# First mixer, latents: sums of squares on VectorE, heads' norms written later, conditioning pieces at program order

## Chip, cores and metric

The kernel runs on one core of a Trainium2 chip. The metric is the device time of one execution, in microseconds (us). The kernel before was timed three times; its median is 1766.79 us. The engines are called by the names that the profile uses: PE (TensorE), DVE (VectorE), ACT (ScalarE), POOL (GpSimd) and SP (SyncE, which here only issues DMAs).

## What is computed

The reference is a diffusion backbone of two layers over 512 latent and 256 context tokens (768 together), with a model width of 1024. The first layer mixes tokens with two kinds of attention side by side: multi-head latent attention and grouped-query attention. Cut to what matters here:

```python
def rmsnorm(x, g):
    return x * lax.rsqrt(jnp.mean(x * x, axis=-1, keepdims=True) + EPS) * g

# conditioning: 6 x 1024 values per layer, each a dot product of length 1024
mod = jnp.dot(jax.nn.silu(c), ada_w[layer]) + ada_b[layer]
# one input projection, cut into: latent q (384), latent kv (256), k_rope (32),
# grouped-query q (512), k (128), v (128)
cq, ckv, kr, gq, gk, gv = split_cols(jnp.dot(h, w_in), EVEN_SPLITS)
q = apply_rope(rmsnorm(gq per head of 64, g_gq))       # 8 heads
k = apply_rope(rmsnorm(gk per head of 64, g_gk))       # 2 heads
# the latents cq and ckv are normalised over their whole width, then projected up
```

After the mixer comes a gated feed-forward block, then the second layer; the output is the latent stream.

## The kernel before, in words

Matrices are multiplied in three passes: each operand is split into a rounded high part and a remainder (`split`, L39: ACT copies the high part at L42, DVE subtracts at L43), and high x high, low x high and high x low are summed in PSUM. Weights come in pieces of at most 1024 columns (`weights`, L59): a DMA from SP's queue into a raw tile `wr` (two buffers), then `wh` on ACT and `wl` on DVE (three buffers each). A raw buffer is free again when its `wl` is made.

The tile framework puts the instructions of each engine (and the DMAs of SP's queue) into a fixed order before the run: among those whose inputs are ready in its plan it takes the one with the best priority, and the priority is the place in the program text unless a block changes it. `ada_piece` (L128) wraps its work in `high_priority(offset=-100000)`; `_ada_piece` (L132) is the same work without the wrapper. One conditioning piece loads 512 KB into a tile `ar` (three buffers, L135), makes two products with row sums on DVE (tiles `junk`, L138, 128x1024 each, one for the latent and one for the context condition) and one small add (L139).

The stretch of the change lies in the first 160 us. `first_norm` (L152, its loop over slices at L241) normalises the input, walks over eight slices k of the width (L221 to L223 make `u`, `hh` and `hl`), runs pieces 12 to 15 for k = 0 to 3 by `_ada_piece`, and accumulates the six 128-token tiles of the grouped-query q in PSUM. Then `even` (L550) goes through these steps in the program text:

1. For six tiles t: `fill()` (L584), which takes one of the pieces 16 to 31; the square on ACT (L586); the rotary products on DVE (L573, L577, from PSUM) with an add on POOL (L581); a sum per head on DVE (L588). The result is `QR`.
2. The weights for k and v, `in_w_gkv`, 288 columns, in three pieces of 3, 3 and 2 slices (L589).
3. For six tiles t: the matmuls into a bank of T, U, R (L592, `tm`, L95), `fill()` (L593), then the same treatment for `KR`, and the split of v (L594 to L601).
4. The inverse root of 60 means per token on DVE (L603, L604): `rg`.
5. Six times: scale `QR[t]` (L607) and `KR[t]` (L609) by `rg` on POOL.
6. For the five column groups c of the latents: weights (`in_w_lat`, L623), 48 matmuls into one of two PSUM buffers `lat` (L626, L85), two `fill()` (L629, L630), the square on ACT into `sa` or `sq` (L632, L635), the add of `sq` to `sa` for c = 1, 2 and 4 (L636, on POOL but for c = 4, one `sq` buffer), and the split into `CQ` or `CK` (L637). The sums over the width are matmuls (L620), at c = 4 and after the loop.
7. Attention: `kprep` transposes `KR` (L680), the q preparation transposes `QR` (L703).

The sixteen pieces are used up by the first twelve `fill()` of steps 1 and 3 and the four of c = 0 and 1.

Of the kernel before, what the change touches and what calls it, by code (L numbers as in the profile page):

```python
# [9 lines left out]
F32 = mybir.dt.float32  # L10
# [7 lines left out]
SUB, ADD, MUL, MAX, MIN = ALU.subtract, ALU.add, ALU.mult, ALU.max, ALU.min  # L18

D = 1024  # L20
NL, NX, T = 512, 256, 768
# [11 lines left out]
class Kernel:  # L33
# [516 lines left out]
    def even(self, hh, hl, acc):  # L550
        nc, i, tc = self.nc, self.i, self.tc
# [4 lines left out]
        TP = tc.alloc_tile_pool(name="inp", bufs=1, reuse_waits="tile", side="right")  # L556
        rest = list(range(16, 32))

        def fill():
            if rest:  # L560
                self.ada_piece(0, rest.pop(0))


        QR = P1.tile([128, 6, 512], F32, tag="QR", name="QR")
        KR = P1.tile([128, 6, 128], F32, tag="KR", name="KR")
# [17 lines left out]
        for t in range(6):  # L583
            fill()  # L584
            sq = TP.tile([128, 512], F32, tag="gsq", name="gsq", bufs=2)
            nc.scalar.square(sq, acc[t])  # L586
            ropemul(QR[:, t], acc[t], Cq, Sq, 8, t)
            nc.vector.tensor_reduce(ssg[:, t, 0:8], sq.rearrange("p (h d) -> p h d", h=8), axis=AX.X, op=ADD)  # L588
        wkv = self.weights(i["w_gkv"], KD, 288)  # L589
        for t in range(6):  # L590
            ps = self.B("TUR")
            self.tm(ps[:, 0:288], wkv, H, KD, t)  # L592
            fill()  # L593
            sq = TP.tile([128, 512], F32, tag="gsq", name="gsq", bufs=2)  # L594
            nc.scalar.square(sq[:, 0:128], ps[:, 0:128])
            ropemul(KR[:, t], ps[:, 0:128], Ck, Sk, 2, t)
            nc.vector.tensor_reduce(ssg[:, t, 8:10], sq[:, 0:128].rearrange("p (h d) -> p h d", h=2), axis=AX.X, op=ADD)
            vs = ps[:, 128:256].rearrange("p (h d) -> p h d", h=2)
            self.split(VG[:, t, :, 0:64], VG[:, t, :, 64:128], vs)
            nc.scalar.activation(sq[:, 128:160], ps[:, 256:288], AF.Square, accum_out=krs[:, t:t + 1])  # L600
            nc.scalar.copy(kr[:, t], ps[:, 256:288])  # L601
        v = self.sm.tile([128, 60], F32, tag="gv", name="gv")
        nc.vector.tensor_scalar(v, ssg.rearrange("p t h -> p (t h)"), 1.0 / 64, EPS, op0=MUL, op1=ADD)  # L603
        rg = self.rsqrt(v, 60, "g").rearrange("p (t h) -> p t h", h=10)  # L604
        for t in range(6):
            a = QR[:, t].rearrange("p (h d) -> p h d", h=8)
            nc.gpsimd.tensor_tensor(a, a, rg[:, t, 0:8].unsqueeze(2).to_broadcast([128, 8, 64]), op=MUL)  # L607
            a = KR[:, t].rearrange("p (h d) -> p h d", h=2)
            nc.gpsimd.tensor_tensor(a, a, rg[:, t, 8:10].unsqueeze(2).to_broadcast([128, 2, 64]), op=MUL)  # L609


        CQ = [P2.tile([128, 3, T], F32R, tag=f"CQ{j}", name="CQ") for j in range(2)]
# [1 line left out]
        sa = [TP.tile([128, T], F32, tag=f"lsa{j}", name="lsa") for j in range(2)]  # L614
        pv = self.B("O")

        def sums(which):
            for t in range(6):
                c = which * 6 + t
                nc.tensor.matmul(pv[:, c:c + 1], sa[which][:, t * 128:(t + 1) * 128], self.o1, start=True, stop=True)  # L620

        for c in range(5):
            w = self.weights(i["w_lat"][c], KD, 128)  # L623
            dst, cc, which = (CQ, c, 0) if c < 3 else (CK, c - 3, 1)
            ps = self.A("lat")
            self.fm([(ps[:, 0:NL], 0, NL), (ps[:, NL:T], NL, NX)], w, H, KD)  # L626
            if c == 4:
                sums(0)
            fill()  # L629
            fill()  # L630
            if cc == 0:
                nc.scalar.square(sa[which], ps[:, 0:T])  # L632
            else:
                sq = TP.tile([128, T], F32, tag="lsq", name="lsq", bufs=1)
                nc.scalar.square(sq, ps[:, 0:T])  # L635
                (nc.vector if c == 4 else nc.gpsimd).tensor_tensor(sa[which], sa[which], sq, op=ADD)  # L636
            self.split(dst[0][:, cc], dst[1][:, cc], ps[:, 0:T])  # L637
        sums(1)
        rl2 = P2.tile([128, 12], F32, tag="rl2", name="rl2")
        rl1 = P2.tile([128, 12], F32, tag="rl1", name="rl1")  # L640

# [215 lines left out]
        for p, ks in ((1, (-3, -2, -1)), (2, (3, 5, 6)), (3, (9, 11, 12))):  # L857
            f, sc = kvpair(p, pds[p])
            c = 6 // len(ks)
# [673 lines left out]
```

## Time and profile before

| what | us |
|---|---|
| median of three runs | 1766.79 |
| lowest and highest run | 1765.13, 1767.14 |
| the profiled execution, its own time | 1765.13 |
| its span in the trace | 1763.3 |
| busy in the span: PE, DVE, ACT, POOL | 1686.3, 1235.4, 733.9, 288.5 |
| mean granted TensorE clock, share of 2.4 GHz | 0.989 |

The span runs from the first to the last instruction in the trace; 1.8 us lie around it. In a timeline row the first number is the start in us, the second the length; "x3" merges three in a row, and a bracket gives the idle time of the engine before it and what ended it. Times in the text are counted from the start of the span.

### The profile page before, as it was taken

The page shows a single profiled execution, that of the slowest core. Times are in us where ns is not written, and L with a number is a line of the kernel's source. Part 1 is how long each engine was busy: PE and PEld are TensorE (multiplying, and loading weights), DVE is VectorE, ACT ScalarE, POOL GpSimd, SP SyncE. Part 2 cuts the span into 40 slices and gives each one's busy share as a digit, 9 for nine tenths or more (in the row PEclk, how much of TensorE's full clock was granted, in tenths as well). Part 3 has the DMA queues.
Part 4 walks back from the last instruction along what each step waited for, and adds up shares of the span by engine and source line. Part 5 has one row for each costly group of instructions (what it writes and reads, how often), then busy time and mean ns, then how long its engine had stood idle before and what let it go on. Part 6 is the DMA issues. An engine that isn't in the chain of part 4 may idle for free.

```text
span 1763.3 us, 25314 instructions
## 1 busy us (share of the span) xinstructions
PE 1686.3 (96%) x9642; PEld 1443.5 (82%) x9642; DVE 1235.4 (70%) x2279; ACT 733.9 (42%) x1363; POOL 288.5 (16%) x337
## 2 busy tenths in 40 slices
PE   7998899999999999999999998999999899999998
PEld 2787787888878888888888877788888798888887
DVE  3997889987787677685758457877778754544444
ACT  3335788997242122221213135645553442232231
POOL 1343454543130000000000015112110300000000
PEclk9998999999999999999999999999999999999999
DMA  7451000004434344342434121111113233233332
GB/s 275 151 165 35 10 12 7 19 1 169 130 133 155 96 134 141 108 156 91 149 96 132 63 95 60 48 59 39 60 37 105 63 108 96 96 96 96 98 101 89
DMA packets 67168, 166.27 MB, mean 94 GB/s; under 512 B 8164, under 2 KB 30692, under 8 KB 66664
## 3 DMA queue, kind: packets, MB, share of 16 engines
q1 hardware_dynamic: 67044, 164.66, 28.7%
q8 instruction: 76, 1.25, 0.3%
q14 instruction: 44, 0.36, 0.1%
q10 hardware_dynamic: 4, 0.01, 0.0%
HBM read 160.44 MB, written 4.20 MB: 93 GB/s over the span
## 4 chain that ended last, share of the span: by engine, by line
PE 72%; DVE 13%; ACT 6%; POOL 4%; issue 3%; DMA 0%; POOLq 0%; DVEq 0%; ACTq 0%; SPq 0%
PE psS L85 30%; PE psT L353 7%; PE psU L353 7%; PE psU L85 4%; PE psR L85 3%; PE psT L85 2%; PE psO L353 2%; PE psR L353 2%; PE S L434 2%; PE psO L479 1%; DVE junk L138 1%; POOL hl L291 1%; PE psR L95 1%; ACT p L442 1%; DVE wl L43 1%
## 5 line engine op out<-in xcount | busy, mean ns | idle before, releaser
L85 PE MATMUL psS<-hl,wh 128*128 128x512 f32 (+1 forms) x992 | 347.2, 351 | 4.4 <-POOL hl L291 4.3
L85 PE MATMUL psS<-hh,wh 128*128 128x512 f32 (+1 forms) x992 | 346.3, 350 | 0.4 <-ACT hh L287 0.4
L85 PE MATMUL psS<-hh,wl 128*128 128x512 f32 (+1 forms) x992 | 346.1, 349 | 0.0
L42 ACT CAST wh<-wr 128x1024 fp32r<-128x1024 f32 (+2 forms) x187 | 193.5, 1036 | 354.3 <-PE psO L353 141.3
L43 DVE TENSOR_TENSOR wl<-wr,wh 128x1024 fp32r<-128x1024 f32 (+2 forms) x187 | 229.0, 1225 | 52.5 <-ACT wh L42 52.2
L85 PEld LDWEIGHTS psS<-hl,wh 128*128 128x128 f32 x992 | 186.4, 188 | 32.7 <-POOL hl L291 7.1
L85 PEld LDWEIGHTS psS<-hh,wh 128*128 128x128 f32 x992 | 186.6, 188 | 26.5 <-ACT hh L287 0.8
L85 PEld LDWEIGHTS psS<-hh,wl 128*128 128x128 f32 x992 | 186.6, 188 | 25.6
L301 DVE SCALAR_TENSOR_TENSOR y<-psS,fcw,y 128x511 f32<-128x511 f32 (+1 forms) x60 | 39.5, 658 | 145.5 <-ACT y L299 145.5
L138 DVE CUSTOM_DVE_ANT_0 y<-ar,cb 128x1024 f32<-128x1024 f32 x112 | 136.4, 1219 | 0.0
L299 ACT ACTIVATE y<-psS,fcb,fcw 128x512 f32<-128x512 f32 (+1 forms) x60 | 40.3, 705 | 207.2 <-PE psS L85 207.2
L271 POOL TENSOR_TENSOR sa<-sa,sq 128x256 f32<-128x256 f32 (+1 forms) x18 | 18.3, 1018 | 643.7 <-ACT sq L270 643.7
L388 DVE SCALAR_TENSOR_TENSOR X<-psU,mod,X 128x512 f32<-128x512 f32 (+1 forms) x69 | 48.0, 695 | 89.4 <-PE psU L353 78.9
L445 POOL TENSOR_SCALAR p<-p,rs 128x768 f32<-128x768 f32 (+1 forms) x96 | 73.9, 776 | 114.4 <-DVE rs L444 75.7
L353 PE MATMUL psT<-ah,wh 128*128 128x512 f32 (+1 forms) x184 | 71.6, 389 | 2.2 <-DVE X L388 1.2
L138 DVE CUSTOM_DVE_ANT_0 junk<-ar,cb 128x1024 f32<-128x1024 f32 x56 | 73.1, 1306 | 0.4
L353 PE MATMUL psU<-ah,wh 128*128 128x512 f32 (+1 forms) x184 | 71.4, 388 | 1.2 <-DVE X L388 1.2
L353 PE MATMUL psT<-ah,wl 128*128 128x512 f32 (+1 forms) x184 | 71.0, 386 | 0.0
L353 PE MATMUL psU<-ah,wl 128*128 128x512 f32 (+1 forms) x184 | 71.0, 386 | 0.0
L335 DVE TENSOR_TENSOR y<-y,psS 128x512 f32<-128x512 f32 (+1 forms) x60 | 34.1, 596 | 52.5 <-PE psS L85 52.5
L353 PE MATMUL psT<-al,wh 128*128 128x512 f32 (+1 forms) x184 | 70.9, 385 | 0.0
L353 PE MATMUL psU<-al,wh 128*128 128x512 f32 (+1 forms) x184 | 70.7, 384 | 0.0
(662 smaller groups left out, 4341.8 us busy)
## 6 DMA issues: line engine op xcount, KB each, us to landing
wr<-in_wup SPq DMA_DIRECT2D x88, 512.0 KB, 3.5
ar<-in_ada SPq DMA_DIRECT2D x84, 512.0 KB, 3.5
wr<-in_wdn SPq DMA_DIRECT2D x44, 512.0 KB, 3.4
pr<-in_adak SPq DMA_DIRECT2D x12, 512.0 KB, 6.6
wr<-in_w_out SPq DMA_DIRECT2D x8, 512.0 KB, 3.5
wr<-in_w_mqk SPq DMA_DIRECT2D x8, 512.0 KB, 3.5
wr<-in_w_mv SPq DMA_DIRECT2D x8, 512.0 KB, 4.3
wr<-in_w_mo SPq DMA_DIRECT2D x8, 512.0 KB, 3.4
```

Of the source, the lines that this page charges most:

```text
L42: nc.scalar.copy(hi, src)
L43: nc.vector.tensor_tensor(lo, src, f32(hi), op=SUB)
L85: nc.tensor.matmul(ps, a, b[:, k, x0:x0 + n], start=i == 0, stop=i == 3 * nk - 1)
L138: nc.vector.tensor_tensor_reduce(out, raw, self.cb[:, c], 1.0, 0.0, MUL, ADD, self.mraw[l][:, n, c:c + 1])
L271: (nc.vector if k % 2 else nc.gpsimd).tensor_tensor(sa[k % 2], sa[k % 2], sq, op=ADD)
L299: nc.scalar.activation(y[:, t0:t0 + n], p, AF.Identity, bias=b, scale=w[1])
L301: nc.vector.scalar_tensor_tensor(y[:, t0 + 1:t0 + n], p[:, 0:n - 1], w[0], y[:, t0 + 1:t0 + n], op0=MUL, op1=ADD)
L335: nc.vector.tensor_tensor(y[:, t0:t0 + n], y[:, t0:t0 + n], p, op=MUL)
L353: nc.tensor.matmul(ps[:, 0:n], x[:, off:off + 128], y[:, t0:t0 + n], start=m == 0, stop=m == 3 * nf - 1)
L388: self.nc.vector.scalar_tensor_tensor(X[:, o, t0:t0 + n], ps[:, 0:n], self.mod[l][:, g0 + o, c:c + 1], X[:, o, t0:t0 + n], op0=MUL, op1=ADD)
L434: nc.tensor.matmul(s[:, c0:c0 + n], q[:, q0:q0 + 128], k[:, k0 + c0:k0 + c0 + n], start=m == 0, stop=m == len(passes) - 1)
L445: nc.gpsimd.tensor_scalar(p[:, 0:nk], p[:, 0:nk], r, 1.0, op0=MUL, op1=MUL)
```

## The change

Three edits in `even`. `fill()` calls `_ada_piece` directly, so the pieces stand in the order at their place in the program text. The loop that scales `QR` and `KR` on POOL is written behind `sums(1)`, and takes all of `KR` before `QR`. The tile `lsq` has two buffers, and all three adds of squares are on DVE.

```diff
         def fill():
             if rest:
-                self.ada_piece(0, rest.pop(0))
+                self._ada_piece(0, rest.pop(0))
...
         rg = self.rsqrt(v, 60, "g").rearrange("p (t h) -> p t h", h=10)
-        for t in range(6):
-            a = QR[:, t].rearrange("p (h d) -> p h d", h=8)
-            nc.gpsimd.tensor_tensor(a, a, rg[:, t, 0:8].unsqueeze(2).to_broadcast([128, 8, 64]), op=MUL)
-            a = KR[:, t].rearrange("p (h d) -> p h d", h=2)
-            nc.gpsimd.tensor_tensor(a, a, rg[:, t, 8:10].unsqueeze(2).to_broadcast([128, 2, 64]), op=MUL)
...
             else:
-                sq = TP.tile([128, T], F32, tag="lsq", name="lsq", bufs=1)
+                sq = TP.tile([128, T], F32, tag="lsq", name="lsq", bufs=2)
                 nc.scalar.square(sq, ps[:, 0:T])
-                (nc.vector if c == 4 else nc.gpsimd).tensor_tensor(sa[which], sa[which], sq, op=ADD)
+                nc.vector.tensor_tensor(sa[which], sa[which], sq, op=ADD)
             self.split(dst[0][:, cc], dst[1][:, cc], ps[:, 0:T])
         sums(1)
+
+        for a, h, r in ((KR, 2, slice(8, 10)), (QR, 8, slice(0, 8))):
+            for t in range(6):
+                z = a[:, t].rearrange("p (h d) -> p h d", h=h)
+                nc.gpsimd.tensor_tensor(z, z, rg[:, t, r].unsqueeze(2).to_broadcast([128, h, 64]), op=MUL)
```

## Rows read from the trace of the kernel before

**Rows 1.** Windows: length, busy PE, PEld, DVE, ACT, POOL; granted clock; DMA share; GB/s.
```profile
83.00:103.00 20.00, 19.33 (x145) 19.08 (x144) 19.81 (x48) 8.35 (x32) 7.86 (x10) 1.00 0.26 83
...
137.40:140.70 3.30, 0.04 (x1) 0.00 (x0) 1.00 (x2) 2.53 (x5) 2.38 (x2) 1.00 0.00 0
140.70:144.70 4.00, 3.98 (x10) 3.13 (x11) 3.97 (x8) 1.90 (x3) 0.16 (x1) 0.57 0.39 71
```

**Rows 2.** Waits from 60 to 160 us: total, times, longest.
```profile
ACT lsq L635 <- POOL lsa L636: 15.1, 1, 15.1
...
PE lat L85 <- DVE CQ L43: 3.3, 1, 3.3
...
PE psT L95 <- ACT kr L601: 0.7, 1, 0.7
...
PE lat L85 <- DVE wl L43: 0.3, 1, 0.3
```

**Rows 3.** Timeline of POOL: a rotary add, the norms, the add of squares.
```profile
84.43 1.30 POOL L581 TENSOR_TENSOR QR<-QR,rt 128x512 f32<-128x512 f32 x1 [0.43 <-DVE rt L577]
...
120.07 2.03 POOL L607 TENSOR_TENSOR QR<-QR,nwy 128x512 f32<-128x512 f32 x1 [10.21 <-DVE mod L139]
...
123.41 1.04 POOL L607 TENSOR_TENSOR QR<-QR,nwy 128x512 f32<-128x512 f32 x1
...
136.32 1.81 POOL L636 TENSOR_TENSOR lsa<-lsa,lsq 128x768 f32<-128x768 f32 x1
```

**Rows 4.** Timeline of PE: end of q, first latent group, restart after the gap.
```profile
83.05 0.29 PE L95 MATMUL psT<-wl,hh 128*128 128x288 f32 x1
...
103.76 0.51 PE L85 MATMUL lat<-hh,wl 128*128 128x512 f32 x1 [0.31 <-DVE wl L43]
...
140.72 0.51 PE L85 MATMUL lat<-hh,wh 128*128 128x512 f32 x1 [3.28 <-DVE CQ L43]
```

**Rows 5.** Timelines of DVE and ACT in first_norm, where pieces have program order.
```profile
41.29 1.80 DVE L223 SCALAR_TENSOR_TENSOR hl<-u,mod,hh 128x512 fp32r<-128x512 f32 x3
...
47.37 1.22 DVE L138 CUSTOM_DVE_ANT_0 junk<-ar,cb 128x1024 f32<-128x1024 f32 x1
...
49.78 0.75 DVE L221 SCALAR_TENSOR_TENSOR u<-X,s,rbs 128x512 f32<-128x512 f32 x1
...
58.56 1.29 ACT L222 ACTIVATE hh<-u,mod 128x512 fp32r<-128x512 f32 x2 [6.88 <-DVE u L221]
```

**Rows 6.** Timeline of DVE from first_norm's end to the k and v tiles, and at 121 us.
```profile
72.05 1.05 DVE L43 TENSOR_TENSOR wl<-wr,wh 128x864 fp32r<-128x864 f32 x1
73.02 1.14 DVE L223 SCALAR_TENSOR_TENSOR hl<-u,mod,hh 128x512 fp32r<-128x512 f32 x2
74.08 1.22 DVE L138 CUSTOM_DVE_ANT_0 junk<-ar,cb 128x1024 f32<-128x1024 f32 x1
...
77.53 1.22 DVE L138 CUSTOM_DVE_ANT_0 junk<-ar,cb 128x1024 f32<-128x1024 f32 x1
...
80.14 1.22 DVE L138 CUSTOM_DVE_ANT_0 junk<-ar,cb 128x1024 f32<-128x1024 f32 x1
...
81.28 0.68 DVE L573 TENSOR_TENSOR QR<-psT,C 128x512 f32<-128x512 f32 x1
...
89.63 0.75 DVE L43 TENSOR_TENSOR wl<-wr,wh 128x576 fp32r<-128x576 f32 x1
...
93.22 1.51 DVE L138 CUSTOM_DVE_ANT_0 junk<-ar,cb 128x1024 f32<-128x1024 f32 x1
...
101.07 1.22 DVE L138 CUSTOM_DVE_ANT_0 junk<-ar,cb 128x1024 f32<-128x1024 f32 x1
...
121.24 1.94 DVE L138 CUSTOM_DVE_ANT_0 junk<-ar,cb 128x1024 f32<-128x1024 f32 x1
```

**Rows 7.** Timeline of SP's queue: two piece loads, the third gkv load.
```profile
66.17 0.91 SPq L135 DMA_DIRECT2D ar<-in_ada  x2
73.17 0.33 SPq L66 DMA_DIRECT2D wr<-in_w_gkv  x1
```

## Prediction before the run

> **What bounds the kernel now.** PE is busy for 1686.3 of the span's 1763.3 us (the table), so a change pays only where PE stands still or runs at the low clock. I read the windows of the first 160 us first. PE stands from 137.4 to 140.7, and then issues only ten matmuls in 4.0 us at a granted clock of 0.57, which is the 1.2 GHz level for most of that window [rows 1]. The waits name the cause: the square of latent group 2 on ACT waits 15.1 us for POOL's add of squares, because there is one `lsq` buffer; the PSUM buffer it reads comes free late, and PE waits 3.3 us [rows 2]. POOL was late because the add at 136.32 stood behind the twelve norm multiplications that began at 120.07 [rows 3]. PE's restart is at 140.72 [rows 4]. Two small PE waits, 0.7 and 0.3 us, stand earlier [rows 2].
>
> Then I looked at DVE in the stage ahead of that. From 83 to 103 us it is busy for 19.81 of 20 us [rows 1]: whatever comes ahead of needed work there delays it. What keeps PE going is the order: ten products of the pieces (16 to 20) lie between 74.08 and 101.07, and after 80.14 the next product is at 93.22, behind all six q tiles [rows 6]. The pieces stand aside now.
>
> **The change, part by part.** *Adds on DVE and a second buffer.* POOL's two adds of 1.81 us [rows 3] become two on DVE. An estimate is 0.9 us each (768 columns; a product over 1024 takes 1.22 [rows 6]). Their cover is the matmuls of the next group, 8.4 us (from 103.76 to 140.72 are four groups and the 3.3 us gap [rows 4]); they cost nothing unless DVE is still full there. ACT no longer waits, so PE's 3.3 us go, and with them the slow restart: 4.0 us at 0.57 lost 4.0 x 0.43 = 1.7 us. Gain 3.3 + 1.7 = 5.0 us.
>
> *Norms written behind the sums.* They took 16.3 us of POOL, from 120.07 to 136.32 [rows 3]. Nothing waits for them before the transposes that open the attention; even begun 20 us later, in a stage that starts later itself, they are done before it ends. Zero, covered by the latents' matmuls.
>
> *Pieces at program order.* This is the term that decides. Where pieces have program order already, in first_norm, they go ahead of later work that is ready: the `u` of slice 2 at 49.78 has had its buffer since the `hl` merged at 41.29, but comes behind the products of pieces 12 and 13 (the one at 47.37 is the first of 13), and ACT later idles 6.88 us for DVE's `u` [rows 5]. In `even`, pieces 16 to 21 stand in the text ahead of the split of the gkv weights, and 22 to 27 between the k tiles.
>
> Their loads move too, ahead of gkv's in SP's queue. Pieces 17 and 18 are issued at 66.17 and will be no later, so 16 to 18 are there when DVE reaches them. The third gkv load waits for a raw buffer and goes at 73.17, just after the first split ends at 73.02 [rows 6, 7]; if that split is late, so is this load, and it is covered as now, by PE taking the first six slices of three k tiles first.
>
> The sum: the hole at 72.05, in which the first gkv split (0.97 us to the next start) runs now, goes to the first half of piece 16, and DVE is through with first_norm at 74.2. Ahead of the gkv split then stand: half of piece 16, 1.25; pieces 17 to 21, five times 2.61 (77.53 to 80.14 is one piece), 13.05; the six q tiles, 16 instructions, of which 14 take 8.35 (81.28 to 89.63), so 9.55; the split itself 0.97. Together 24.8: it ends at 99.0 [rows 6]. PE has begun k and v by 83.05 [rows 4] and will stand until 99.0, 16.0 us. Beside POOL's rotary adds of 1.30 [rows 3] a product is slower: 1.94 instead of 1.21 us beside the norms [rows 3, 6]. Three products fall beside such adds; 3 x 0.73 = 2.2 more, 18.2 us idle (bounds 0 and 3.9, if each waits a whole add).
>
> The Trainium skill, "SBUF — State Buffer", section "Who interferes with whom", says that a VectorE instruction with two SBUF inputs shares a port with GpSimd's reads, and that the later one is blocked until the earlier has ended. By that rule the three products could lose up to 1.30 each, the idle time would be 19.9 us, and the result 1.7 us later. The trace agrees in kind, with less than a full wait: 1.94 us here is 0.73 more, and the norm beside it took 2.03 where another took 1.04.
>
> Behind the stop: a slow restart like that at 140.72, 1.7 us (bounds 0, since PE may keep its clock, and 3.4, since this stop is far longer). The 0.7 us wait in the k tiles goes, as DVE will be ahead there. At the hand-over to the latents PE waits 0.3 us now for the split of the first latent weights; then that split stands behind the last k tile and up to one whole piece: bounds 0.3 and 2.9, I take 2.0, nearer the piece, since pieces 22 to 27 fill DVE up to the last k tile. So +1.7.
>
> Net: 18.2 + 1.7 - 0.7 + 1.7 - 5.0 = 15.9 us. A cross-check: twelve pieces lie ahead of the latents instead of five, on a full DVE: 7 x 2.61 = 18.3, less the 5.0 won: 13.3. If the first two gkv splits slip in early, this count still holds, and PE only stops later. With all lows, 16.0 - 0.7 - 5.0 = 10.3; with all highs, 19.9 + 3.4 - 0.7 + 2.6 - 5.0 = 20.2.
>
> The profiled execution took 1765.13, 1.7 below the median. 1765.1 + 15.9 = **1781.0**; its own range, taking in the median, is 1775.4 to 1787.
>
> **The rivals.** *Faster: the gkv splits stay ahead.* Place: DVE between 72 and 83 us. If the order put all three gkv splits there or between q tiles, and later pieces in holes, PE keeps its pace and only the gain remains: 1765.1 - 5.0 = 1760.1. It decides whether the two splits of 864 columns start before 83.05. For it: in the plan by which the order is made, loads may take longer than on the chip, so that pieces are not ready and the split gets its turn. Against: three pieces can lie in `ar` before 74, which fill DVE until the q tiles are ready, and the first_norm rows show the order at work. 17%.
>
> *No change.* A stop of only some 5 us, because pieces 19 to 21 come late from memory (three `ar` buffers, each free only after its two products), so that the splits go in between, pays back the gain: 1765.1, within 3.5 us. 8%.
>
> *The change doesn't do what it says.* The POOL wait could stay if DVE's adds stood behind pieces. But pieces 28 to 31 belong to groups 0 and 1, and the wait is at group 2; it only takes from the gain, and is in the ranges.
>
> **How the numbers follow.** The stop of k and v has 75%, 1781.0. About 0.2%, 3.5 us, is what a measurement of this kernel can tell from no change. The faster case gives 0.17, the one without change 0.08, the slower one 0.75. A range that leaves out only the faster case runs from 1763.5 (the low edge of no change) to 1787.
>
> **What would show it.** Right: in the profile after, the products of 17 to 21 stand between the q tiles; the `wl` of 864 columns starts near 98; PE waits some 16 to 20 us for it at 83, at the low clock afterwards; the latents begin 18 to 22 us later than 103.76 [rows 4], run without a gap for 42 us (five times 8.4), and ACT's 15.1 us wait is gone. Wrong: if the split with 864 columns starts before 83, or if PE's wait there is under 5 us, the first rival holds; if ACT or PE still stops at group 2, then the gain was misjudged; if the attention's first transposes wait for POOL, the norms were not covered.

## The result, and the profile after

The kernel after takes 1780.2 us (median of 4 runs, 1779.67 to 1781.66); the kernel before, 1765.96 (4 runs, 1763.71 to 1767.14). The ratio is 1.008, with a 95% interval of 1.0068 to 1.0092: slower by 14.2 us. The forecast was 1781.0, and the profiled execution took 1779.95 with a span of 1778.2, 14.9 us more than before. Further down, one execution of the kernel with the norms moved alone took 9293 us; it stands in no median and no comparison.

The waits from 60 to 180 us show what went and what came (total, times, longest):

```profile
ACT lsq L630 <- PE lat L85: 17.9, 3, 6.3
...
PE psT L95 <- DVE wl L43: 11.1, 1, 11.1
...
POOL KR L638 <- DVE mod L139: 10.3, 1, 10.3
...
PE lat L85 <- DVE wl L43: 4.5, 1, 4.5
...
PE psT L95 <- ACT kr L601: 1.1, 1, 1.1
```

ACT's wait of 15.1 us for POOL's add and PE's 3.3 us behind it [rows 2] are gone; the square now waits for PE, which is as it should be. In their place PE waits 11.1 us for a split of weights, and the wait of 0.3 us at the hand-over to the latents has become 4.5. The timeline of PE from 100 to 130 us has the places:

```profile
102.27 0.61 PE L95 MATMUL psT<-wl,hh 128*128 128x288 f32 x1 [11.10 <-DVE wl L43]
...
107.39 0.61 PE L95 MATMUL psT<-wh,hh 128*128 128x288 f32 x1 [1.15 <-ACT kr L601]
...
124.58 0.80 PE L85 MATMUL lat<-hh,wl 128*128 128x512 f32 x1 [4.54 <-DVE wl L43]
```

The stop lies in the k and v tiles, as forecast, and the latents begin at 124.58 instead of 103.76 [rows 4], 20.8 us later. What PE waited for is in the timeline of DVE:

```profile
72.56 1.22 DVE L138 CUSTOM_DVE_ANT_0 junk<-ar,cb 128x1024 f32<-128x1024 f32 x1
...
75.90 1.05 DVE L43 TENSOR_TENSOR wl<-wr,wh 128x864 fp32r<-128x864 f32 x1
...
78.09 1.05 DVE L43 TENSOR_TENSOR wl<-wr,wh 128x864 fp32r<-128x864 f32 x1
...
85.12 1.95 DVE L138 CUSTOM_DVE_ANT_0 junk<-ar,cb 128x1024 f32<-128x1024 f32 x1
...
88.86 1.94 DVE L138 CUSTOM_DVE_ANT_0 junk<-ar,cb 128x1024 f32<-128x1024 f32 x1
...
93.75 1.83 DVE L138 CUSTOM_DVE_ANT_0 junk<-ar,cb 128x1024 f32<-128x1024 f32 x1
...
99.67 1.21 DVE L138 CUSTOM_DVE_ANT_0 junk<-ar,cb 128x1024 f32<-128x1024 f32 x1
...
101.48 0.74 DVE L43 TENSOR_TENSOR wl<-wr,wh 128x576 fp32r<-128x576 f32 x1
...
121.71 1.21 DVE L138 CUSTOM_DVE_ANT_0 junk<-ar,cb 128x1024 f32<-128x1024 f32 x1
...
123.32 1.21 DVE L43 TENSOR_TENSOR wl<-wr,wh 128x1024 fp32r<-128x1024 f32 x1
```

Twelve products stand from 72.56 to 99.67, among the q tiles, where five stood up to 80.14 and the next came at 93.22 [rows 6]; from 102.15 to 121.71 come twelve more. That makes 24 products, twelve pieces, ahead of the first latent weights. The two `wl` of 864 columns, which the forecast had put near 98 us, did get in early, at 75.90 and 78.09; the third, of 576, runs at 101.48, behind all q tiles and pieces, 11.9 us later than before [rows 6], although its load was issued at 77.03:

```profile
76.01 0.33 SPq L135 DMA_DIRECT2D ar<-in_ada  x1
77.03 1.09 SPq L66 DMA_DIRECT2D wr<-in_w_gkv  x1
```

The windows (columns as in [rows 1]) show the clock behind each stop:

```profile
91.00:102.20 11.20, 0.17 (x2) 0.00 (x0) 11.20 (x22) 0.60 (x1) 1.26 (x1) 0.67 0.33 98
102.20:107.40 5.20, 3.98 (x16) 3.63 (x16) 5.17 (x13) 1.14 (x7) 0.46 (x1) 0.50 0.80 258
107.40:113.00 5.60, 5.60 (x27) 5.60 (x28) 5.60 (x16) 0.90 (x6) 0.92 (x2) 0.61 0.46 143
...
124.50:128.50 4.00, 3.92 (x9) 3.14 (x10) 4.00 (x9) 0.36 (x3) 2.63 (x2) 0.50 0.75 249
...
136.00:168.30 32.30, 32.30 (x190) 28.40 (x188) 12.32 (x17) 8.44 (x13) 11.90 (x12) 1.00 0.14 44
```

DVE is busy for all of the 11.20 us in which PE stands. After both stops the granted clock is 0.50, the 1.2 GHz level. From 136 on PE runs the latents without a gap at 1.00, and DVE, which has used up its pieces, is busy for 12.3 of 32.3 us. The norms, POOL's 11.90 us in that window, end before the attention's first transposes, for which PE waits on DVE alone: their multiplications are at 138.23 and 142.35.

```profile
138.23 4.16 POOL L638 TENSOR_TENSOR KR<-KR,nwy 128x128 f32<-128x128 f32 x6 [10.31 <-DVE mod L139]
142.35 7.78 POOL L638 TENSOR_TENSOR QR<-QR,nwy 128x512 f32<-128x512 f32 x6
```

**Where the time went.** Behind the latents' last matmul PE goes on at 168.09, before at 150.75: +17.3. The pieces of that: the stop 11.1; the low clock behind it, 3.98 x 0.50 + 5.60 x 0.39 = 4.2; the hand-over 4.5 - 0.3 = 4.2 and its low clock, 3.92 x 0.50 = 2.0; the k tiles' wait 1.15 - 0.67 = 0.5; the gap at group 2 and its slow restart, -5.0. Sum 17.0. Another 0.5 is older than the change: a load that goes at 30.82 in the trace before goes at 31.32 in this one. That makes 17.5, 0.2 more than measured. The attention's first score matmul is 17.35 later (159.45 to 176.80), its last output matmul 14.7 (422.22 to 436.92), and the feed-forward block begins 14.7 later: some 2.6 us come back within the attention. Some 0.8 of them lie near its start: the matmul at 171.56 before stands at 188.09 after, 16.53 later, and in the first 6.55 us the clock is 0.57 before and 0.75 after. Some 1.1 more come behind a wait that both kernels have, after which only the kernel before ran at the low clock (the last section shows it). The rest was not followed up. The first 6.55 us, before:

```profile
159.45:166.00 6.55, 6.55 (x23) 6.10 (x24) 3.90 (x10) 3.87 (x7) 0.91 (x1) 0.57 0.00 0
```

After:

```profile
176.80:183.35 6.55, 6.53 (x27) 5.68 (x28) 4.38 (x11) 3.71 (x7) 0.91 (x1) 0.75 0.00 0
```

### The profile page after: what moved, and what is told of

It is laid out like the page before. It is cut to its first block, busy times and chain, and to the rows that moved or that the text cites. A ratio compares the mean times of both kernels' runs of the same rounds, so it can differ in the third digit from the quotient of the medians.

```text
span 1778.2 us, 25310 instructions
## 1 busy us (share of the span) xinstructions
PE 1688.5 (95%) x9642; PEld 1444.4 (81%) x9642; DVE 1236.0 (70%) x2281; ACT 733.8 (41%) x1363; POOL 280.6 (16%) x335
## 4 chain that ended last, share of the span: by engine, by line
PE 72%; DVE 14%; ACT 7%; POOL 3%; issue 3%; DMA 0%; POOLq 0%; DVEq 0%; ACTq 0%
PE psS L85 30%; PE psT L353 7%; PE psU L353 7%; PE psU L85 4%; PE psR L85 3%; PE lat L85 2%; PE psT L85 2%; PE psO L353 2%; PE psR L353 2%; DVE junk L138 2%; PE S L434 2%; POOL hl L291 1%; PE psO L479 1%; ACT p L442 1%; PE psR L95 1%
## 5 line engine op out<-in xcount | busy, mean ns | idle before, releaser
L271 POOL TENSOR_TENSOR sa<-sa,sq 128x256 f32<-128x256 f32 (+1 forms) x18 | 18.3, 1018 | 643.7 <-ACT sq L270 643.7
```

What stands on the lines that cost most here:

```text
L271: (nc.vector if k % 2 else nc.gpsimd).tensor_tensor(sa[k % 2], sa[k % 2], sq, op=ADD)
```

## Experiments

The theory: the pieces at program order carry the whole loss, by filling DVE ahead of work that PE needs, and the other two edits win what the gap at group 2 cost. The rival: what decides is where a single split stands in DVE's order, so that an earlier split cures it.

**The pieces put back, the rest as changed** (against the kernel after):

```diff
-                self._ada_piece(0, rest.pop(0))
+                self.ada_piece(0, rest.pop(0))
```

> The changed kernel with its pieces put back to low priority; adds on DVE, two buffers and the later norms stay. Theory (the loss is the pieces ahead of needed work on a full DVE): PE's wait at latent group 2 is gone with its slow restart, the gkv splits stand where they were, the time is 5.0 us below the kernel before, 1760 to 1762. Rival (part of the loss comes from the adds on DVE or from norms that are done too late): the time is above the kernel before, 1768 or more, and the attention's first transposes wait for POOL.

1762.65 us, ratio 0.9974 (0.9963 to 0.9985). As expected in sign, but 4.1 us below the kernel before on that chip where 5.0 was expected, just outside 1760 to 1762. **The pieces alone**, in the kernel before:

```diff
-                self.ada_piece(0, rest.pop(0))
+                self._ada_piece(0, rest.pop(0))
```

> The kernel before with the pieces at program order as the only edit; POOL keeps its adds and its norms in their old place. Theory: the same stops as in the changed kernel (11 us for the third gkv split, 4.5 us for the first latent weights). The norms start late, near 138, and take some 12 us, so POOL is free by 151, when the square of group 2 wants its buffer: no wait there even without the other two edits, 1779 to 1782. Rival (the other two edits carry a part of the loss): 1776 or less. Third outcome: the POOL wait stays as it was, then 1785.

1781.6 us, ratio 1.0083 (1.0069 to 1.0097). PE's waits are those of the kernel after, 11.1 and 4.5 us; at group 2 it does not stop, although POOL's adds are still late (150.83, 153.60). ACT waits for them, but for 6.1 us instead of 15.1 [rows 2]:

```profile
ACT lsq L635 <- POOL lsa L636: 6.1, 1, 6.1
```

DVE is through with the pieces when the norms begin, and the twelve norms take 11.2 us of POOL (139.68 to 150.83) instead of 16.3; the latents themselves come later, too. The one line carries the whole loss. Beside it the other two edits are worth nothing that can be measured (the ratios 1.0083 and 1.008 lie in each other's intervals): the later latents have no gap left to close.

**The k and v weights written ahead of the q tiles** (against the kernel after):

```diff
+        wkv = self.weights(i["w_gkv"], KD, 288)
         for t in range(6):
             fill()
...
-        wkv = self.weights(i["w_gkv"], KD, 288)
```

> The changed kernel with the gkv weights written ahead of the loop over the six q tiles, so that their splits and loads come before pieces 16 to 21. Theory (a full DVE, the number of pieces ahead of the latents counts): PE's stop of 11 us for the third split goes, but PE stops for DVE later, at the k tiles or at the first latent weights; the latents start at 118 or later instead of 124.6, the time is 1772 to 1778. Rival (the one late split is the cause): the stop and its slow clock go for good, some 15 us, 1765 or less.

1783.44 us, ratio 1.0092 (1.0076 to 1.0108). The place in the text does set the split's turn: the third goes from 101.48 to 84.30. But nothing is won, and the expected 1772 to 1778 missed. Timeline of DVE in this run:

```profile
84.30 0.76 DVE L43 TENSOR_TENSOR wl<-wr,wh 128x576 fp32r<-128x576 f32 x1
...
106.84 0.28 DVE L43 TENSOR_TENSOR VG<-psT,VG 128x128 fp32r<-128x128 f32 x1
```

And of PE:

```profile
107.57 0.61 PE L95 MATMUL psT<-wh,hh 128*128 128x288 f32 x1 [14.46 <-ACT kr L601]
```

PE finishes three k tiles early and then stands 14.5 us for the first of the three PSUM banks, which is free only when DVE has worked through the q tiles' pieces and come to that k tile (its v is split at 106.84). The queue on DVE is as long; only the thing waited for changed, and the latents begin at 123.36 instead of 124.58. So the rival falls.

**Program order for the q tiles' pieces only, and for the k tiles' and latents' only** (against the kernel after, `_ada_piece` with `fill(True)` alone):

```diff
-        def fill():
+        def fill(own=False):
...
-                self._ada_piece(0, rest.pop(0))
+                (self._ada_piece if own else self.ada_piece)(0, rest.pop(0))
...
         for t in range(6):
-            fill()
+            fill(True)
```

The other has `own=True` there and `fill(False)` in the q loop.

> The changed kernel with program order for the pieces of the q tiles alone (16 to 21); those at the k tiles and the latents have low priority. Theory: PE's stop of about 11 us for the third gkv split stays, since it comes from 16 to 21; the 4.5 us for the first latent weights and its slow restart (1.9 us) go, since 22 to 27 stand aside: 1773 to 1775. Rival (the pieces at the k tiles cost the most): under 1768.

> The changed kernel with low priority for the pieces of the q tiles (16 to 21) and program order for those at the k tiles and the latents (22 to 31). Theory (pieces ahead of needed work on a full DVE): no stop for the third gkv split, but waits at the k tiles and at the first latent weights, since three low pieces hold the load buffers and are run first and six more go ahead of the k tiles: four pieces more ahead of the latents than in the kernel before, 10 us, less the gain of 4: 1770 to 1775. Rival (only the q tiles' pieces hurt): 1763 or less, like the run with all pieces at low priority.

The first: 1776.93 us, ratio 1.0056 (1.004 to 1.0071), 2 us above the expected range. The 11 us stop stays, the hand-over's wait is gone:

```profile
104.44 0.61 PE L95 MATMUL psT<-wl,hh 128*128 128x288 f32 x1 [11.07 <-DVE wl L43]
```

The second: 1775.04 us, ratio 1.005 (1.0037 to 1.0063), at the upper edge of the expected range. No stop in the k tiles, but the pieces of the q tiles, standing aside, are now done beside the latents with all the others, and those have program order there:

```profile
124.31 1.01 PE L680 MATMUL psT<-ident,KR 128*64 128x128 f32 x3 [1.23 <-POOL KR L638]
...
132.98 0.79 PE L85 MATMUL lat<-hh,wl 128*128 128x512 f32 x1 [2.72 <-DVE wl L43]
```

The first of these lines shows that here the later norms are not covered: the transposes of `KR` stand among the latents' matmuls in PE's order, and PE waits for POOL's norms four times, 3.9 us in all.

Each half of the line loses. Against the kernel before on the same chip the halves are 10.2 and 8.3 us slower, both together 14.2, and the kernel with all pieces standing aside is 3.5 faster (below). So the halves lose 13.7 and 11.8 us, which don't add up to what both lose, 17.7.

**The other two edits, one at a time.** The adds on DVE with two buffers, and nothing else:

```diff
-                sq = TP.tile([128, T], F32, tag="lsq", name="lsq", bufs=1)
+                sq = TP.tile([128, T], F32, tag="lsq", name="lsq", bufs=2)
...
-                (nc.vector if c == 4 else nc.gpsimd).tensor_tensor(sa[which], sa[which], sq, op=ADD)
+                nc.vector.tensor_tensor(sa[which], sa[which], sq, op=ADD)
```

> The kernel before with the adds on DVE and the second buffer as the only edits; norms and pieces as before. Theory: this alone takes away the wait for POOL at group 2 and its slow restart, so 4 us below the kernel before, like the run with all pieces low. Rival (the later norms are needed too): no gain, within 1.5 us of the kernel before.

> The kernel before with the norms written behind the sums as the only edit; POOL keeps its adds, one buffer. Theory: POOL's adds now come ahead of the norms in its order, or behind one of them at most, so the wait of 15 us for the buffer shrinks below 3 us and PE does not stop at group 2: 3 to 5 us below the kernel before. Rival (the adds still stand behind the twelve norms, which are ready first): no gain.

> The norms written later as the only edit, once more, for its trace. POOL's order in the run with two buffers and POOL's adds had the adds behind nine and behind twelve norms. Theory: one buffer and this order make ACT wait for the add of group 1 for about as long as the norms take, some 10 us, less than the 15 us of the kernel before, and PE's stop at group 2 is shorter than 3.3 us but not gone.

The adds: 1763.51 us, ratio 0.9981 (0.9972 to 0.9989). The norms' loop alone, moved as in the diff of the change: 1764.06 us, 0.9991 (0.9982 to 0.9999), 2.7 us below the kernel before on that chip where 3 to 5 was expected; the trace is that of a second look (one run, 1763.42). Timeline of POOL there:

```profile
126.45 6.06 POOL L638 TENSOR_TENSOR QR<-QR,nwy 128x512 f32<-128x512 f32 x3
132.48 2.89 POOL L631 TENSOR_TENSOR lsa<-lsa,lsq 128x768 f32<-128x768 f32 x1
```

The add gets in between the norms at 132.48 instead of 136.32 [rows 3], but takes 2.89 us instead of 1.81. ACT still waits 12.1 us for it, where the first expectation said under 3 and the second some 10, and PE's stop at group 2 is all but gone (0.3 us). Either edit alone closes the gap; together they win 4.1 (the first experiment) or 3.5 (a second look at it, below), not the sum of 3.2 and 2.7.

**Two buffers and later norms, but the adds left on POOL** (against the first experiment's kernel):

```diff
-                nc.vector.tensor_tensor(sa[which], sa[which], sq, op=ADD)
+                (nc.vector if c == 4 else nc.gpsimd).tensor_tensor(sa[which], sa[which], sq, op=ADD)
```

> Norms written behind the sums and two buffers, pieces at low priority, but the adds of groups 1 and 2 stay on POOL. In the run with the adds on DVE, DVE was full up to the end of the latents, its adds took up to 1.79 us beside POOL's norms, and PE waited 1.2 us for the last add and then ran at the low clock. Theory: taking the two adds (some 3 us) off DVE ends that wait, 1 to 2 us below that run, 1760 to 1762. Rival (DVE's share there costs nothing): the same time as that run.

1766.86 us, ratio 0.9999 (0.9989 to 1.0009): the expectation fell. Timelines of POOL and of PE:

```profile
132.30 2.90 POOL L631 TENSOR_TENSOR lsa<-lsa,lsq 128x768 f32<-128x768 f32 x1
...
139.79 2.83 POOL L631 TENSOR_TENSOR lsa<-lsa,lsq 128x768 f32<-128x768 f32 x1
```

```profile
151.32 2.56 PE L615 MATMUL psO<-o,lsa 128*128 128x1 f32 x12 [2.35 <-DVE lsa L631]
```

The gap at group 2 is closed here too, but PE waits 2.35 us for the last add, which stands on DVE behind the last pieces. In the next run the wait is 1.2 us, and the two timelines of DVE show why. Here POOL's norms and adds reach to 142.62 instead of 137.27, and what stands beside them on DVE is slower:

```profile
136.86 2.06 DVE L138 CUSTOM_DVE_ANT_0 junk<-ar,cb 128x1024 f32<-128x1024 f32 x1
...
140.84 1.80 DVE L139 TENSOR_TENSOR mod<-mraw,adab 128x2 f32<-128x2 f32 x1
```

In the next run such a product takes 1.22 us there and the small add 0.15. So DVE loses beside POOL what the two adds no longer take of it, and more, and the last add starts at 150.31 instead of 149.22. That is about 1 us; the medians differ by some 3. The profiled execution (1762.87) was 4.0 us faster than its median, so its trace does not show the rest.

**Fewer pieces in the stretch.** The gain of 5.0 at group 2 had come out as 4.1 in the first experiment. A second look at the first experiment's kernel says why. Timeline of PE, then windows:

> The run with all pieces at low priority once more, beside the two that move pieces, on the same chip: 3 to 5 us below the kernel before.

```profile
145.75 1.39 PE L615 MATMUL psO<-o,lsa 128*128 128x1 f32 x12
...
150.23 1.50 PE L615 MATMUL psO<-o,lsa 128*128 128x1 f32 x12 [1.18 <-DVE lsa L631]
...
156.25 0.80 PE L434 MATMUL S<-KH,QE 128*128 128x512 f32 x1 [1.59 <-DVE QE L709]
```

```profile
104.00:129.00 25.00, 25.00 (x144) 21.87 (x145) 24.93 (x49) 6.76 (x12) 11.51 (x10) 1.00 0.62 204
129.00:150.00 21.00, 20.05 (x123) 17.64 (x121) 20.76 (x35) 8.04 (x13) 8.26 (x5) 1.00 0.32 98
150.00:158.00 8.00, 5.48 (x25) 4.42 (x26) 6.58 (x20) 2.81 (x6) 0.95 (x2) 0.61 0.00 1
```

The latents take 41.85 us (103.90 to 145.75) where they took 47.0, so 5.1 are won; the first score matmul is only 3.2 earlier, since PE waits 1.2 us for the last add, DVE being full until 150, and the clock is 0.61 after that. So pieces 28 to 31, and then 24 to 31, were moved on to the output projection (against the first experiment's kernel):

```diff
-        rest = list(range(16, 32))
+        rest = list(range(16, 28))
...
-                todo = list(range(32, 40))
+                todo = list(range(28, 40))
```

> The run with all pieces at low priority (adds on DVE, two buffers, later norms), with the last four pieces of the stage (28 to 31) left to the output projection, whose list of pieces becomes 28 to 39. Theory (DVE is full up to the end of the latents, and 2 us of the 5 won are given back because the last add stands behind the last products): 10.4 us less on DVE there, the wait of 1.2 us for the last add goes, and PE's clock at the start of the attention is higher; the projection has DVE idle for 8.8 of 20 us between 460 and 480: 1 to 3 us below the run with all pieces low, 1759 to 1762. Rival (the projection pays for it): the same as that run or slower.

> The same with the last eight pieces (24 to 31) left to the output projection: 21 us of DVE work moved. Theory: it does not fit into the idle time of the projection (some 10 us), so the second norm waits for its shifts and the gain is lost there: slower than with four moved, 1763 to 1768. Rival (the projection hides eight as well): as with four, or 1 us better.

1767.74 us, ratio 1.0003 (0.9995 to 1.0012), and 1776.48 us, 1.0057 (1.0045 to 1.007): both expectations fell. With four moved, the wait for the last add is gone and the attention ends 1.7 us earlier (417.32, against 419.00 in the second look), but the feed-forward block begins 4.1 later (492.06, against 487.94). Waits of PE from 440 to 500 us, and a window, with four moved:

```profile
PE psR L276 <- DVE X L388: 2.7, 1, 2.7
```

```profile
460.00:480.00 20.00, 17.31 (x85) 14.60 (x85) 18.76 (x36) 2.21 (x4) 2.17 (x2) 0.99 0.35 106
```

In the second look DVE is busy for 9.95 us of that window and PE for 20.00. With eight moved, the block's first matmul comes at 502.33, after a wait of 7.9 us for ACT. The output projection has no room for more pieces, although DVE was idle for half of that window.

The kernel that beats both: pieces standing aside, adds on DVE with two buffers, norms later. In the second look it took 1763.6 us (11 runs), ratio to before 0.9979 (0.997 to 0.9988), beside 1767.05 for the kernel before on that chip.

## Why the prediction was right, and where its steps were off

*Adds and second buffer, gain 5.0.* The gap is gone and the latents run without a stop, as forecast, but that is not this edit's doing: with the pieces alone the gap is gone as well, and that kernel is as slow (1781.6). So beside the pieces the edit is worth nothing that can be measured, and the -5.0 of the sum comes with the pieces' line alone. Where the pieces stand aside the term is right for the latents (5.1 in the second look); what it left out is that DVE is still full behind the last products, so 1.2 us and some low clock are given back there. By itself the edit won 3.2. The prediction had named that condition ("unless DVE is still full there").

*Norms later, zero.* Right in this kernel: covered by a wide margin. With the pieces of the q tiles alone standing aside it was not.

*Pieces at program order.* Right in kind and in the sum: their terms were 18.2 + 1.7 - 0.7 + 1.7 = 20.9, and 22.0 came out (11.1 + 4.2 + 4.2 + 2.0 + 0.5). The whole forecast was +15.9, measured +14.9. The terms erred in both directions:

- "The split itself 0.97. Together 24.8: it ends at 99.0." The step that failed. The first two splits got in early, so PE did not stop at 83 but went on to 91 and stopped at the third: 11.1 us instead of 18.2. The prediction allowed for it ("PE only stops later"), but it also named a split of 864 columns before 83 as the sign that its first rival, the faster kernel, holds. The sign came and the rival did not: for that the third split had to be early too. Why these two got in is open. The loads of pieces 17 and 18 were out by 63.91, before those of the gkv weights at 64.33; by the third experiment, text order does move a split, so the two pieces were probably not ready in the plan by which the order is made.
- "A slow restart like that at 140.72, 1.7 us." Mis-sized: 4.2 us behind the stop, beyond the bound of 3.4, and 2.0 behind the hand-over, a second restart that the sum had no term for.
- The hand-over: 4.5, where 2.0 was taken and 2.9 was the bound. PE is through with the last k tile at 119.05, but DVE comes to it only at 122.86, behind products that start at 118.71, 120.36 and 121.71, and to the split at 123.32. DVE was not "ahead there", and for the same reason the k tiles' wait did not go (1.15 instead of 0).
- Contention, 3 x 0.73 = 2.2: three products beside rotary adds took 1.95, 1.94 and 1.83 instead of 1.21, so 0.74 + 0.73 + 0.62 = 2.1. These adds are, in POOL's timeline:

```profile
84.69 1.29 POOL L581 TENSOR_TENSOR QR<-QR,rt 128x512 f32<-128x512 f32 x1 [0.42 <-DVE rt L577]
...
88.43 1.30 POOL L581 TENSOR_TENSOR QR<-QR,rt 128x512 f32<-128x512 f32 x1 [2.44 <-DVE rt L577]
...
93.24 1.26 POOL L581 TENSOR_TENSOR QR<-QR,rt 128x512 f32<-128x512 f32 x1 [3.52 <-DVE rt L577]
```

When the products began (85.12, 88.86, 93.75), 0.86, 0.87 and 0.75 us of the adds were still to run. By the rule of the Trainium skill, "SBUF — State Buffer", section "Who interferes with whom", the later one waits until the earlier has ended, so each product would lose that rest. The trace agrees to within 0.14 us. The prediction took a whole add of 1.30 for it and read the row at 121.24 as "less than a full wait"; of the norm beside that product, too, only 0.86 us were left when it began, and it lost 0.73.

Why the sum held although PE stopped elsewhere: the cross-check counted what stands on a full DVE ahead of the latents. It counted seven pieces more, 18.3 us. The trace shows 24 products ahead of the first latent split instead of ten, which is just seven pieces more. With the contention of 2.1 and the 0.5 by which this execution was late beforehand that makes 20.9, and the latents do begin 20.8 us later (the forecast said 18 to 22). So it is no luck that the stop, taken 7.1 us too long, and the later terms, too short, nearly cancel. That the whole came within 1.0 is luck in part: the 2.6 us that come back inside the attention had no term, and without them it would have been +17.5, still in the range.

## What to carry to other kernels

Where the engine that feeds PE is full, count all its work ahead of the next stage: that gives the delay even where the order in between is guessed wrongly, and moving one needed instruction forward only changes what PE waits for. Filler belongs below everything that PE waits for, and it needs a stage with room: here the latents had some, the output projection had none. Close a gap and look at the next hand-over: 5.1 us won at group 2 were 3.2 at the attention's first matmul.

## What was not expected of the hardware

How long the low clock lasts does not follow from the length of the stop alone. After 3.3 us without matmuls the clock was 0.57 for 4.0 us [rows 1]; after 11.1 us, 0.50 for 5.2 us and 0.61 for 5.6 more, with another wait of 1.15 us between; after 4.5 us, 0.50 for 4.0 and then 0.98. Nor does a stop of one length always bring it. In the attention PE waits 2.98 us for DVE's split of `ptl`, before and after alike; in the stretch that ends with this wait it was busy for 4.69 of 9.40 us before (from 200.00) and for 4.95 of 9.96 after (from 216.00). Windows from the end of that wait, before:

```profile
209.40:212.00 2.60, 2.60 (x12) 2.60 (x13) 1.94 (x5) 0.70 (x3) 1.84 (x3) 0.51 0.00 0
```

After:

```profile
225.96:228.56 2.60, 2.60 (x22) 2.60 (x23) 2.52 (x9) 1.48 (x5) 1.84 (x3) 1.00 0.00 0
```

The same wait is followed by the 1.2 GHz level in one execution and by 2.4 GHz in the other; what decides it, these traces do not show.

DVE and POOL slow each other both ways. POOL's add of squares took 1.81 us in the kernel before and 2.89 or 2.90 beside a product on DVE that had 1.19 us still to run, so it lost all but some 0.1 of that; a DVE add of the same size, 0.96 us where POOL was idle, took 1.79 beside POOL's norms (first experiment):

```profile
135.59 1.79 DVE L631 TENSOR_TENSOR lsa<-lsa,lsq 128x768 f32<-128x768 f32 x1
```
